# Last head's scores ahead of the output splits, the recurrence in three parts, and two gate products ahead of the memory rows

## The chip, the core and the metric

The kernel runs on one core of one Trainium2 chip. Its engines work side by side, each with a queue that is executed in order: TensorE (PE) multiplies, and PEld is its weight load; VectorE (DVE), ScalarE (ACT) and GpSimd (POOL) work on tiles; SyncE (SP) issues most of the DMAs, ScalarE some. The metric is the time of one execution in microseconds of device time, as the median of several executions. All times below are microseconds unless marked ns.

## What is computed

A sequence of 512 rows of width 1024 (fp32) goes through two blocks, each of two layers.

First block. Layer 0 mixes with dilated attention: 8 heads, and for each head three groups of keys (window and stride 128/1, 512/4, 2048/16) whose outputs are joined by the softmax of their log sums; then a convolving feed-forward network of width 3072. Layer 1 mixes with a gated linear recurrence (RG-LRU) of width 1024, and then has the same kind of network. The recurrence, as the reference has it:

```
r = sigmoid(xr @ ga_w + ga_b);  i = sigmoid(xr @ gx_w + gx_b)
log_a = LRU_C * r * log_sigmoid(lam);  a = exp(log_a)
b = sqrt(max(-expm1(2*log_a), 0)) * i * xb
hs = scan(h_t = a_t*h_(t-1) + b_t);  out = (hs * gelu(gb)) @ w_out
```

Second block, twice: the normed rows are projected, and three branches work on the result: sparse attention of 8 heads (nsa), attention with a decay of 8 heads (fox), and attention over 256 memory rows with 4 heads (memory). Each branch's output goes through a matrix of its own and is multiplied with a sigmoid gate, and the sum goes through a last matrix and is added to the rows:

```
mem_kv = rmsnorm(mem) @ w_mem_kv;  o_m = attention(rmsnorm(q), rmsnorm(k), v) * silu(...)
u = g0*(o_a @ w_branch_a) + g1*(o_b @ w_branch_b) + g2*(o_m @ w_branch_m)
x = x + u @ w_out
```

## The kernel before

Every fp32 matrix product is made of three products of rounded halves (`mm3`, lines 45 to 47): each operand is split into a high part (a cast on ACT) and the rest (a subtraction on DVE), by `split` at line 204. A weight is loaded as 128x1024 values by SP into one of two `ws` tiles and split into one of four pairs `wh`, `wl` (`wunit`, line 212). PSUM is used in four kinds of banks: `acc` (3), `sc` (2), `tr` (2), `pv` (1).

The Python code only sets which instructions there are. A planner orders them on each engine when the program is built, from times that it simulates, so that later work can be pulled into a gap; at run time each queue is in order. `issue_after`, and the helper `behind` around it, tell the planner to place what is written inside the block behind a given instruction on the same engine. `DMA` issues stand in the queue of the engine that issues them.

The three places of the change:

* The end of the attention. `DilatedHead.scores(qk, order)` makes the scores of a head in one of two orders of the rows: four tiles, each with a minimum on DVE (line 109) and an exponential on ACT (line 111). It then writes its statistics to DRAM (`dx<-W`, line 112) and reads the other order's back (`W<-dx`, line 113), both on SP. `normalize` joins the groups (lines 122 to 129) and scales the probabilities on POOL (line 133); `values` transposes them (lines 143, 154) and multiplies with the values. Head 7 is the last: after its scores come the splits of `oT`, the heads' output, for heads 0 to 6 (`hH`, `hL`<-`oT`), the first half of the product with `w_o` (`tm`), and inside it `hold`, which runs `normalize` and `values` of head 7 behind head 6's split and the last weight split.
* The recurrence. `lru_layer` walks `LRU_STEPS`: a number n is `front(n)`, which takes two columns of x from the input product, convolves them (lines 580, 582), splits them, and makes two gates for each (line 722); a range is `recur` over these columns, with Exp and Tanh, then Ln, then Exp on ACT (lines 730, 731, 737, 740) and seven DVE operations a column (lines 744 to 751); each "v" takes one column of gb out of its `acc` bank (line 761). Eight columns of gb in all; the last four stay in their banks till the gelu (line 769), which is placed behind the last Exp of the last recurrence. Then the halves of hs*gate go into the product with `w_out`.
* The start of the second block, in each of its two layers. `memory` loads small vectors, the gain `gm` and the memory rows, norms the rows (lines 309, 312), and takes the four query tiles from `z2`. After two query tiles have been issued, the normed memory rows are transposed (`turned`, line 320) between them; then follow the product with `w_mem_kv` and the four heads. `weave` runs a branch and lets `branch` (gate products of 24 matmuls in two steps, and a product of 12 with the branch's output in one step) fill in, at the steps that `PLANS` lists.

Of the kernel before, what the change touches and what calls it, by code (L numbers as in the profile page):

```python
# [12 lines left out]
AF = mybir.ActivationFunctionType  # L13
OP = mybir.AluOpType
# [4 lines left out]
D = 1024  # L19
NT = T // 128  # L20
KD = D // 128
EPS = 1e-6
NEG = -1e30
BIG = 3e38
# [4 lines left out]
SEC_BUFS = {"st": 7, "ws": 2, "w": 4, "o": 6, "P": 5, "pt": 4, "zc": 3, "hst": 4, "fox_t": 4, "of": 2, "rt": 2, "sl": 2, "mt": 2, "cst": 2, "ct": 2}  # L29
LRU_BUFS = 24  # L30
NORMALIZE_AFTER, VALUES_AFTER = 5, 6
LRU_STEPS = (0, 1, 2, range(4), "v", 3, range(4, 8), "vvv")
PLANS = ((16,),
         (8, 13, 13, 14, 15, 18, 19, 19, 22, 22, 25, 26, 26, 27, 27, 28, 28, 29, 29, 35, 35, 37, 38, 39),
         (1, 5, 5, 8, 8, 10, 12, 15, 16, 17, 19, 21, 32, 32, 34, 35, 38))
TURN_BANKS = (("acc", "sc"), ("acc", "sc"), ("sc", "tr"), ("tr", "pv"))
# [23 lines left out]
class DilatedHead:  # L60
# [23 lines left out]
    def scores(self, qk, order):  # L84
        n, nc = self.n, self.n.nc
        own = self.W[:, order, 0]
        ps = None
        for t in range(NT):
            ts = slice(t * 128, (t + 1) * 128)
            P = self.rows(order, t)  # L90
            N = P.shape[-1]
            if order:

                S = n.bank("sc").rearrange("p (g u c) -> p u g c", g=2, u=2)
                for g in (1, 2):
                    q = qk[g]
                    nc.tensor.matmul(S[:, :, g - 1], q[:, 0, ts], q[:, 2:4, ts], start=True, stop=False)
                    nc.tensor.matmul(S[:, 0, g - 1], q[:, 1, ts], q[:, 2, ts], start=False, stop=True)
                two = lambda x: x.rearrange("p (g c) -> p g c", g=2)
                nc.vector.tensor_tensor(two(P), S[:, 1], two(self.bias[:, 256:512]), op=OP.add)  # L100
                S, bias, P3 = S[:, 0], two(P), two(P)
            else:
                if t % 2 == 0:
                    ps = n.bank("sc")
                S = ps[:, t % 2 * 256:t % 2 * 256 + N]
                q, ks = qk[0], slice((t + 1) * 128 - N, (t + 1) * 128)
                mm3(nc, S, q[:, 0, ts], q[:, 1, ts], q[:, 2, ks], q[:, 3, ks], True, True)
                bias, P3 = self.bias[:, 256 - N:256], P
            nc.vector.tensor_tensor_reduce(out=P3, in0=S, in1=bias, scale=-1.0, scalar=BIG, op0=OP.add, op1=OP.min,
                                           accum_out=own[:, 0, t:t + 1])  # L110
            nc.scalar.activation(P, P, AF.Exp, bias=own[:, 0, t:t + 1], scale=-1.0, accum_out=own[:, 1, t:t + 1])
        nc.sync.dma_start(self.in_dram(order, order), own)
        nc.sync.dma_start(self.W[:, 1 - order, 1], self.in_dram(order, 1 - order))

    def normalize(self):

# [52 lines left out]
class Net:  # L169
# [287 lines left out]
    def dilated_attention(self, qkv, oT):  # L457

        i, ap = self.i, self.ap
        btab = self.btab  # L460
        vectors = self.vectors()
        later, vs, done = [], {}, []
        n = 0

        def after(steps, f, *args):

            later.append((n + steps, f, args))

        def load(hp):
            vs[hp] = self.dilated_values(hp)  # L470

        def values(a):
            a.values(vs[a.hd // 2], a.hd % 2, oT)

        def normalize(a):

            with behind(self.tc, *done):
                a.normalize()

        def due(end=False):  # L480
            for x in [x for x in later if end or x[0] <= n]:
                later.remove(x)
                x[1](*x[2])

        for hd in range(8):
            qk = {}
            a = None
            for g in (1, 2, 0):
                t4 = ap.tile([128, 4, T], F32R, tag="qk", bufs=4, name="qk")
                for u in range(2):  # L490
                    ps = next(qkv)
                    n += 1
# [12 lines left out]
            if hd < 7:  # L505
                after(1, a.scores, qk, 0)
            if hd % 2 == 0:
                after(0, load, hd // 2)
            if hd < 7:
                after(NORMALIZE_AFTER, normalize, a)  # L510
                after(VALUES_AFTER, values, a)
        a.scores(qk, 0)
        due(True)

        def last(ins):
            done[:] = ins
            normalize(a)
            values(a)
        return last

    def first_rows(self, g):

# [23 lines left out]
    def attn_layer(self, g_next, nxt):  # L546
        i, tc = self.i, self.tc
        with tc.tile_pool(name="attO", bufs=1) as self.op, tc.tile_pool(name="attA", bufs=2) as self.ap:
            ap, self.ep = self.ap, self.op
            vs = self.post_vectors(i["norm_mix_post"][0], g_next)  # L550
            self.ep = ap
            oT = self.op.tile([128, KD, T], F32, tag="oT", bufs=1, name="oT")
            last = self.dilated_attention(self.attn_qkv(self.h), oT)
            oh = self.new_h()
            for k in range(KD - 1):
                done = self.split(oh[0][:, k], oh[1][:, k], oT[:, k])

            def hold():
                last((*done, *self.last_split))
                self.split(oh[0][:, KD - 1], oh[1][:, KD - 1], oT[:, KD - 1])  # L560

            free = {}

            def spare(i):
                if i // 4 not in free:
# [222 lines left out]
    def state(self, shape, dt=F32R):  # L788
        return self.lt("st", shape, dt)

    def small_bc(self, row, n, name):
        t = self.lt(name, [128, n])
        self.nc.sync.dma_start(t, row[None, :].to_broadcast([128, n]))
        return t

    def rope_tables(self, g, scale=1.0):
# [160 lines left out]
    def second_layer(self, l, z2):  # L957
        nc, i, tc = self.nc, self.i, self.tc
        w_in, h = i["w_in_2"][l], self.h
        with tc.tile_pool(name=f"sec{l}", bufs=1) as self.lp:  # L960
            lp = self.lp
            u, o_m, o_a, o_b = [], [], [], []
            br = [self.branch(l, h, o, i[f"w_branch_{x}_2"][l], b, u) for o, x, b in ((o_m, "m", 2), (o_a, "a", 0), (o_b, "b", 1))]
            self.weave(self.memory(l, h, w_in, z2, o_m), br[0], PLANS[0])
            self.weave(self.nsa(l, h, w_in, o_a), itertools.chain(br[0], br[1]), PLANS[1])
            self.weave(br[0])
            self.weave(self.fox(l, h, w_in, o_b), itertools.chain(br[1], br[2]), PLANS[2])
# [40 lines left out]
    def branch(self, l, h, o, w, b, u):  # L1008
# [9 lines left out]
        def gate(m):  # L1018
# [1 line left out]
            wh, wl = self.wunit(wg[:, :, c:c + 128])  # L1020
            pg = self.bank()
            for k in range(KD):
                mm3(nc, pg, wh[:, k], wl[:, k], h[0][:, k], h[1][:, k], k == 0, k == KD - 1)
                if k == KD // 2 - 1:
                    yield
            t = self.lt("mt", [128, T])
# [347 lines left out]
            nc.sync.dma_start(K[o:o + 2, e::2], self.cd[1, :, 4 * hf + e:4 * hf + 4:2])  # L1374


    def memory(self, l, h, w_in, z2, os):
        nc, i, lp = self.nc, self.i, self.lp
        lh, ll = self.rows(h)
        gq = self.small_bc(i["mem_q_norm_2"][l], 128, "gq")  # L1380
        gk = self.small_bc(i["mem_k_norm_2"][l], 128, "gk0")
        gm = self.lt("pt", [128, D])
        nc.sync.dma_start(gm, i["mem_norm_g_2"][l][None, :].to_broadcast([128, D]))
        mH, mL = self.state([128, KD, 256]), self.state([128, KD, 256])
        rows = []
        for t in range(2):
            mt, xn = self.lt("pt", [128, D]), self.lt("o", [128, D])
            nc.sync.dma_start(mt, i["mem_2"][0, t * 128:(t + 1) * 128])
            rows.append(self.normed(mt, gm, (xn[:, :512], xn[:, 512:], xn)))
        Q = [self.state([128, 2, 2, T]) for _ in range(2)]  # L1390
        for t, ps in enumerate(z2):
            if t >= 2:
                self.turned(rows[t - 2], (mH, mL), t - 2)
            cs = slice(t * 128, (t + 1) * 128)
            for c in range(2):
                zc = self.lt("zc", [128, 256])
# [1 line left out]
                qn = self.head_norm(zc, 2, 128)  # L1398
                nc.vector.scalar_tensor_tensor(qn, qn, 128 ** -0.5, gq[:, None, :].to_broadcast([128, 2, 128]), op0=OP.mult, op1=OP.mult)
                pt = self.transposed([qn[:, a] for a in range(2)])  # L1400
                self.split(Q[c][:, 0, :, cs], Q[c][:, 1, :, cs], pt[:, :256].rearrange("p (h q) -> p h q", h=2))
            yield
        wkv = i["w_mem_kv_2"][l]
        mlh, mll = self.rows((mH, mL))
        K = self.state([128, 2, 4, 256])
# [136 lines left out]
```

## Time and profile before

| | |
|---|---|
| Median of 3 runs | 2842.91 (2842.14 to 2843.55) |
| The profiled execution | 2847.33 |
| Its span, from the first to the last instruction | 2845.2 |
| PE busy | 2752.4 (97%), 14493 matmuls |
| DVE, ACT, POOL busy | 1655.0 (58%), 1285.5 (45%), 509.2 (18%) |
| Mean granted clock of TensorE | 0.988 of full speed |

The profile is of one execution. Busy time of an engine is the time in which at least one of its instructions ran; consecutive matmuls overlap in it, so a matmul's duration is longer than its distance to the next. A row names the line of the kernel, the engine, the operation, and what it writes and reads (`hH<-oT`).

### The profile page before, as it was taken

To read this page: it belongs to the slowest core of one execution; us is meant where nothing else is said; L and a number is where in the kernel's file an instruction comes from. 1 tells how busy PE (TensorE), PEld (TensorE's weight loads), DVE (VectorE), ACT (ScalarE), POOL (GpSimd) and SP (SyncE) were. 2 spreads that over 40 slices of the span, in tenths; PEclk is the share of its full clock that TensorE was granted. 3 is DMA by queue.
4 is the path that set the end of the run, shared out by engine and by line. 5 is a ranking of instruction groups with operands and counts; after the bars stand their busy time and mean duration, and the time that the engine had idled before them with its cause. 6 is when DMAs were issued, how large, how long until landed. Compare 5 with 4: busy or idle time off the path is not lost.

```text
span 2845.2 us, 39405 instructions
## 1 busy us (share of the span) xinstructions
PE 2752.4 (97%) x14493; PEld 2338.7 (82%) x14493; DVE 1655.0 (58%) x3306; ACT 1285.5 (45%) x2518; POOL 509.2 (18%) x682
## 2 busy tenths in 40 slices
PE   7999999799999998999998999999999899999999
PEld 6788888688888887888887898789878798788987
DVE  3245555555542678555425687776744677777753
ACT  3234344344432465444323554666533554665542
POOL 0001101111100000111001242333320242333420
PEclk9999999899999999999999999999999999999999
DMA  5553443333332343433323424122234423113233
GB/s 172 171 169 86 104 94 86 118 111 97 97 126 96 112 122 108 126 96 97 126 97 114 125 74 109 38 54 75 71 93 141 137 70 109 34 46 84 71 93 107
DMA packets 386071, 288.52 MB, mean 101 GB/s; under 512 B 33576, under 2 KB 339496, under 8 KB 385880
## 3 DMA queue, kind: packets, MB, share of 16 engines
q1 hardware_dynamic: 376752, 268.94, 32.9%
q10 hardware_dynamic: 9128, 17.07, 1.6%
q8 instruction: 115, 1.88, 0.3%
q14 instruction: 76, 0.62, 0.1%
HBM read 266.86 MB, written 21.20 MB: 101 GB/s over the span
## 4 chain that ended last, share of the span: by engine, by line
PE 82%; DVE 8%; DMA 4%; ACT 3%; issue 2%; POOL 1%; SPq 0%; ACTq 0%; DVEq 0%; POOLq 0%
PE acc L45 20%; PE acc L46 20%; PE acc L47 20%; PE tr L856 2%; PE sc L45 2%; PE sc L46 2%; PE sc L47 2%; DVE wl L204 2%; PE pv L916 2%; PE tr L45 2%; PE tr L47 1%; PE tr L46 1%; PE pv L46 1%; PE pv L47 1%; DMA ws<-in_attn_w_qkv_dram 1%
## 5 line engine op out<-in xcount | busy, mean ns | idle before, releaser
L204 DVE TENSOR_TENSOR wl<-ws,wh 128x1024 fp32r<-128x1024 f32 (+2 forms) x476 | 563.9, 1186 | 686.8 <-ACT wh L204 680.8
L204 ACT CAST wh<-ws 128x1024 fp32r<-128x1024 f32 (+2 forms) x476 | 469.5, 987 | 819.7 <-PE acc L46 303.6
L45 PE MATMUL acc<-hH,wh 128*128 128x512 f32 (+1 forms) x1928 | 742.3, 386 | 12.2 <-ACT gate L769 6.2
L46 PE MATMUL acc<-hL,wh 128*128 128x512 f32 (+1 forms) x1928 | 741.3, 385 | 1.5 <-DVE hL L204 1.2
L47 PE MATMUL acc<-hH,wl 128*128 128x512 f32 (+1 forms) x1928 | 739.5, 384 | 1.0 <-DVE wl L204 1.0
L45 PEld LDWEIGHTS acc<-hH,wh 128*128 128x128 f32 x1928 | 363.3, 189 | 83.6 <-ACT gate L769 6.6
L47 PEld LDWEIGHTS acc<-hH,wl 128*128 128x128 f32 x1928 | 363.9, 189 | 69.2 <-DVE wl L204 1.5
L46 PEld LDWEIGHTS acc<-hL,wh 128*128 128x128 f32 x1928 | 364.1, 189 | 68.4 <-DVE hL L204 2.5
L45 PE MATMUL acc<-wh,hH 128*128 128x256 f32 (+3 forms) x864 | 267.3, 312 | 5.4 <-ACT hH L204 4.1
L46 PE MATMUL acc<-wl,hH 128*128 128x256 f32 (+3 forms) x864 | 266.9, 310 | 2.3 <-DVE wl L204 2.3
L47 PE MATMUL acc<-wh,hL 128*128 128x256 f32 (+3 forms) x864 | 264.9, 309 | 0.1
L45 PEld LDWEIGHTS acc<-wh,hH 128*128 128x128 f32 x864 | 165.6, 192 | 14.5 <-ACT hH L204 4.5
L46 PEld LDWEIGHTS acc<-wl,hH 128*128 128x128 f32 x864 | 165.7, 192 | 11.9 <-DVE wl L204 3.7
L47 PEld LDWEIGHTS acc<-wh,hL 128*128 128x128 f32 x864 | 165.3, 191 | 7.4 <-DVE hL L204 0.4
L645 POOL TENSOR_TENSOR cv<-cv 128x512 f32<-128x512 f32 x48 | 62.0, 1292 | 465.1 <-DVE cv L582 448.4
L582 DVE SCALAR_TENSOR_TENSOR cv<-acc,cw,cv 128x511 f32<-128x511 f32 (+1 forms) x192 | 142.5, 746 | 3.2
L856 PE MATMUL tr<-ident,P 128*128 128x128 f32 x720 | 123.3, 277 | 10.7 <-DVE pt L204 5.2
L817 POOL TENSOR_TENSOR hst<-hst,mhalf 128x4 f32<-128x4 f32 (+2 forms) x90 | 91.0, 1017 | 223.5 <-DVE hst L816 221.7
L889 ACT ACTIVATE P<-P,soft 128x128 f32<-128x128 f32 (+1 forms) x192 | 108.1, 563 | 49.9 <-DVE soft L888 45.7
L888 DVE CUSTOM_DVE_ANT_0 P<-sc,causal 128x128 f32<-128x128 f32 (+1 forms) x192 | 92.9, 486 | 45.8 <-PE tr L856 31.5
L891 POOL TENSOR_SCALAR P<-P,soft,ngate 128x128 f32<-128x128 f32 (+3 forms) x128 | 83.9, 658 | 153.6 <-DVE soft L890 117.5
L204 DVE TENSOR_TENSOR pt<-tr,pt 128x128 fp32r<-128x128 f32 (+2 forms) x224 | 104.1, 474 | 11.8 <-ACT pt L204 10.4
(452 smaller groups left out, 4770.1 us busy)
## 6 DMA issues: line engine op xcount, KB each, us to landing
ws<-in_w_in_dram SPq DMA_DIRECT2D x116, 512.0 KB
ws<-in_ffn_w_up_dram SPq DMA_DIRECT2D x96, 512.0 KB
ws<-in_attn_w_qkv_dram SPq DMA_DIRECT2D x72, 512.0 KB
ws<-in_ffn_w_down_dram SPq DMA_DIRECT2D x48, 512.0 KB
x<-x ACTq DMA_DIRECT2D x16, 512.0 KB
ws<-in_lru_w_in_dram SPq DMA_DIRECT2D x16, 512.0 KB
ws<-in_w_mem_kv_dram SPq DMA_DIRECT2D x16, 512.0 KB
ws<-in_w_out_dram SPq DMA_DIRECT2D x16, 512.0 KB
```

The lines of the kernel that those rows point to most:

```text
L45: nc.tensor.matmul(out, lh, rh, start=start, stop=False)
L46: nc.tensor.matmul(out, lh, rl, start=False, stop=False)
L47: return nc.tensor.matmul(out, ll, rh, start=False, stop=stop)
L204: return nc.scalar.copy(hi, src), (eng or nc.vector).tensor_tensor(lo, src, hi.bitcast(F32), op=OP.subtract)
L582: nc.vector.scalar_tensor_tensor(dst[:, s:], ps[:, :T - s], cw(taps - 1 - s), dst[:, s:], op0=OP.mult, op1=OP.add)
L645: nc.gpsimd.tensor_tensor(g, g, v, op=OP.mult)
L817: nc.gpsimd.tensor_tensor(st[:, 1], st[:, 0], self.mhalf[:rows, :nh], op=OP.pow)
L856: self.nc.tensor.transpose(ps[:, a * 128:(a + 1) * 128], s, self.ident)
L888: nc.vector.tensor_tensor_reduce(out=P, in0=S, in1=self.causal[:, 512 - n:512], scale=-1.0, scalar=BIG, op0=OP.add, op1=OP.min, accum_out=m)
L889: nc.scalar.activation(P, P, AF.Exp, bias=m, scale=-1.0, accum_out=s)
L891: nc.gpsimd.tensor_scalar(P, P, r, mult, op0=OP.mult, op1=OP.mult)
L916: nc.tensor.matmul(ps[:, lo:256], v(j), p[:, j, lo:], start=first and j == 0 and u == 0, stop=last and j == nj - 1 and u == 1)
```

## The change

1. `LRU_STEPS` runs three recurrences (columns 0 to 3 after the second front, 4 and 5 after the third, 6 and 7 after the fourth) in place of two (0 to 3 after the third front, 4 to 7 after the fourth). The columns of the input product keep their order.
2. The splits of `oT` of heads 0 to 6 are placed behind the last minimum and the last exponential of head 7's scores. `normalize` of head 7 is placed behind the split of head 6 alone. Head 7's two reads `W<-dx` are issued by POOL in place of SP.
3. In `memory` the two small vectors, the two tiles of memory rows and `gm` are loaded from ACT's queue in place of SP's, the rows ahead of `gm`. The rows are normed behind the last split of the queries, and transposed behind the last matmul of the second gate product: four steps of `branch` (two gate products of 24 matmuls) are run between the queries and the memory rows. The one fill step inside the memory branch (at its step 16) goes; the other plans stay, so that each finds the branch three steps further on.

```diff
-LRU_STEPS = (0, 1, 2, range(4), "v", 3, range(4, 8), "vvv")
-PLANS = ((16,),
+LRU_STEPS = (0, 1, range(4), 2, range(4, 6), "v", 3, range(6, 8), "vvv")
+PLANS = ((),
...
-            nc.vector.tensor_tensor_reduce(out=P3, in0=S, in1=bias, scale=-1.0, scalar=BIG, op0=OP.add, op1=OP.min,
-                                           accum_out=own[:, 0, t:t + 1])
-            nc.scalar.activation(P, P, AF.Exp, bias=own[:, 0, t:t + 1], scale=-1.0, accum_out=own[:, 1, t:t + 1])
+            ends = (nc.vector.tensor_tensor_reduce(out=P3, in0=S, in1=bias, scale=-1.0, scalar=BIG, op0=OP.add, op1=OP.min,
+                                                   accum_out=own[:, 0, t:t + 1]),
+                    nc.scalar.activation(P, P, AF.Exp, bias=own[:, 0, t:t + 1], scale=-1.0, accum_out=own[:, 1, t:t + 1]))
         nc.sync.dma_start(self.in_dram(order, order), own)
-        nc.sync.dma_start(self.W[:, 1 - order, 1], self.in_dram(order, 1 - order))
+        (nc.gpsimd if self.hd == 7 else nc.sync).dma_start(self.W[:, 1 - order, 1], self.in_dram(order, 1 - order))
+        return ends
...
-            for k in range(KD - 1):
-                done = self.split(oh[0][:, k], oh[1][:, k], oT[:, k])
+            with behind(tc, *ends):
+                for k in range(KD - 1):
+                    done = self.split(oh[0][:, k], oh[1][:, k], oT[:, k])
...
-                last((*done, *self.last_split))
+                last(done)
...
-            self.weave(self.memory(l, h, w_in, z2, o_m), br[0], PLANS[0])
+            self.weave(self.memory(l, h, w_in, z2, o_m, br[0]), br[0], PLANS[0])
...
-        for t in range(2):
-            mt, xn = self.lt("pt", [128, D]), self.lt("o", [128, D])
-            nc.sync.dma_start(mt, i["mem_2"][0, t * 128:(t + 1) * 128])
-            rows.append(self.normed(mt, gm, (xn[:, :512], xn[:, 512:], xn)))
         Q = [self.state([128, 2, 2, T]) for _ in range(2)]
         for t, ps in enumerate(z2):
-            if t >= 2:
-                self.turned(rows[t - 2], (mH, mL), t - 2)
...
+        for n in range(4):
+            next(fill)
+        with behind(self.tc, *ends):
+            rows = []
+            for mt in mts:
+                xn = self.lt("o", [128, D])
+                rows.append(self.normed(mt, gm, (xn[:, :512], xn[:, 512:], xn)))
+        with behind(self.tc, self.last_gate):
+            for t in range(2):
+                self.turned(rows[t], (mH, mL), t)
```

## Rows read from the trace of the kernel before

**Rows 1.** The page, its first part: busy time, share of the span, instructions.

```profile
PE 2752.4 (97%) x14493; PEld 2338.7 (82%) x14493; DVE 1655.0 (58%) x3306; ACT 1285.5 (45%) x2518; POOL 509.2 (18%) x682
```

**Rows 2.** Waits of PE: who was waited for, us in total, times, longest.

```profile
PE tr L143 <- POOL PA L133: 7.0, 1, 7.0
...
PE acc L320 <- ACT o L309: 4.3, 1, 4.3
...
PE acc L320 <- DVE o L312: 3.4, 1, 3.4
```

**Rows 3.** Busy time (x instructions) of PE, PEld, DVE, ACT, POOL by stretch; clock; DMA.

```profile
480.00:535.00 55.00, 42.26 (x208) 35.46 (x208) 26.11 (x55) 20.09 (x44) 3.76 (x9) 0.84 0.25 77
...
1020.00:1070.00 50.00, 48.80 (x214) 39.78 (x214) 38.41 (x56) 40.94 (x55) 0.00 (x0) 1.00 0.44 136
1070.00:1085.00 15.00, 8.79 (x31) 6.76 (x30) 14.82 (x22) 12.07 (x20) 0.00 (x0) 0.77 0.26 89
...
1549.00:1566.00 17.00, 9.11 (x28) 6.44 (x27) 12.90 (x36) 8.42 (x23) 6.28 (x9) 0.60 0.29 104
...
2203.00:2218.00 15.00, 8.53 (x34) 6.35 (x33) 11.58 (x33) 9.00 (x23) 6.65 (x9) 0.77 0.39 119
```

**Rows 4.** Timeline at the attention's end: start, us, engine, line, what.

```profile
479.17 0.93 PE L143 MATMUL tr<-ident,PA 128*128 128x128 f32 x7
480.80 0.45 PE L45 MATMUL acc<-wh,hH 128*128 128x512 f32 x1
...
479.44 2.17 ACT L204 CAST hH<-oT 128x512 fp32r<-128x512 f32 x4
...
483.50 0.68 DVE L204 TENSOR_TENSOR qk<-acc,qk 128x512 fp32r<-128x512 f32 x1
...
495.38 0.49 ACT L111 ACTIVATE PA<-PA,W 128x256 f32<-128x256 f32 x1
...
496.00 0.37 SPq L112 DMA_DIRECT2D dx<-W  x1
505.65 0.36 SPq L113 DMA_DIRECT2D W<-dx  x1
...
509.74 0.17 DVE L122 TENSOR_TENSOR c<-W 128x8 f32<-128x8 f32 x1 [4.08 <-DMA W<-dx]
...
512.33 0.21 ACT L125 ACTIVATE c<-c 128x16 f32<-128x16 f32 x1
...
514.60 1.74 POOL L133 TENSOR_SCALAR PA<-PA,c 128x128 f32<-128x128 f32 x4 [34.41 <-DVE c L129]
...
515.03 2.06 PE L143 MATMUL tr<-ident,PA 128*128 128x128 f32 x7 [7.00 <-POOL PA L133]
```

**Rows 5.** Timeline of the recurrence, on ACT, DVE and PE.

```profile
1023.50 1.28 ACT L730 ACT_TABLE_LOAD   x1
...
1052.91 2.93 ACT L730 ACTIVATE a<-th,lrul 128x512 f32<-128x512 f32 x4
...
1072.67 1.28 ACT L769 ACT_TABLE_LOAD   x1
1073.97 2.19 ACT L769 ACTIVATE gate<-gate 128x512 f32<-128x512 f32 x4
...
1041.42 0.68 DVE L761 COPY gate<-acc 128x512 f32<-128x512 f32 x1
...
1076.69 0.79 PE L45 MATMUL acc<-hH,wh 128*128 128x512 f32 x1 [6.21 <-ACT gate L769]
```

**Rows 6.** Timeline of the first memory branch's start, on SP and PE.

```profile
1549.89 0.91 SPq L1388 DMA_DIRECT2D pt<-in_mem_dram  x2
...
1560.58 0.78 PE L45 MATMUL acc<-wh,hH 128*128 128x512 f32 x1
...
1565.42 0.52 PE L47 MATMUL acc<-wh,hL 128*128 128x512 f32 x1
```

**Rows 7.** Timeline of the fox branch's end, on PE.

```profile
2091.00 0.95 PE L45 MATMUL acc<-o,wh 128*128 128x512 f32 x2 [2.29 <-ACT o L204]
```

More of the change, by code (lines that the diff above doesn't have):

```diff
@@ L511, in dilated_attention @@
                 after(VALUES_AFTER, values, a)
-        a.scores(qk, 0)
+        ends = a.scores(qk, 0)
         due(True)
@@ L518, in last @@
             values(a)
-        return last
+        return last, ends
     def first_rows(self, g):
@@ L552, in attn_layer @@
             oT = self.op.tile([128, KD, T], F32, tag="oT", bufs=1, name="oT")
-            last = self.dilated_attention(self.attn_qkv(self.h), oT)
+            last, ends = self.dilated_attention(self.attn_qkv(self.h), oT)
             oh = self.new_h()
-            for k in range(KD - 1):
-                done = self.split(oh[0][:, k], oh[1][:, k], oT[:, k])
+            with behind(tc, *ends):
+                for k in range(KD - 1):
+                    done = self.split(oh[0][:, k], oh[1][:, k], oT[:, k])
             def hold():
-                last((*done, *self.last_split))
+                last(done)
                 self.split(oh[0][:, KD - 1], oh[1][:, KD - 1], oT[:, KD - 1])
@@ L789, in state, with small_bc @@
         return self.lt("st", shape, dt)
-    def small_bc(self, row, n, name):
+    def small_bc(self, row, n, name, eng=None):
         t = self.lt(name, [128, n])
-        self.nc.sync.dma_start(t, row[None, :].to_broadcast([128, n]))
+        (eng or self.nc.sync).dma_start(t, row[None, :].to_broadcast([128, n]))
         return t
@@ L1022, in gate @@
             for k in range(KD):
-                mm3(nc, pg, wh[:, k], wl[:, k], h[0][:, k], h[1][:, k], k == 0, k == KD - 1)
+                self.last_gate = mm3(nc, pg, wh[:, k], wl[:, k], h[0][:, k], h[1][:, k], k == 0, k == KD - 1)
                 if k == KD // 2 - 1:
@@ L1374, in decay_keys, with memory @@
             nc.sync.dma_start(K[o:o + 2, e::2], self.cd[1, :, 4 * hf + e:4 * hf + 4:2])
-    def memory(self, l, h, w_in, z2, os):
+    def memory(self, l, h, w_in, z2, os, fill):
         nc, i, lp = self.nc, self.i, self.lp
         lh, ll = self.rows(h)
-        gq = self.small_bc(i["mem_q_norm_2"][l], 128, "gq")
-        gk = self.small_bc(i["mem_k_norm_2"][l], 128, "gk0")
+        gq = self.small_bc(i["mem_q_norm_2"][l], 128, "gq", nc.scalar)
+        gk = self.small_bc(i["mem_k_norm_2"][l], 128, "gk0", nc.scalar)
         gm = self.lt("pt", [128, D])
-        nc.sync.dma_start(gm, i["mem_norm_g_2"][l][None, :].to_broadcast([128, D]))
+        mts = [self.lt("pt", [128, D]) for _ in range(2)]
+        for t in range(2):
+            nc.scalar.dma_start(mts[t], i["mem_2"][0, t * 128:(t + 1) * 128])
+        nc.scalar.dma_start(gm, i["mem_norm_g_2"][l][None, :].to_broadcast([128, D]))
         mH, mL = self.state([128, KD, 256]), self.state([128, KD, 256])
-        rows = []
-        for t in range(2):
-            mt, xn = self.lt("pt", [128, D]), self.lt("o", [128, D])
-            nc.sync.dma_start(mt, i["mem_2"][0, t * 128:(t + 1) * 128])
-            rows.append(self.normed(mt, gm, (xn[:, :512], xn[:, 512:], xn)))
         Q = [self.state([128, 2, 2, T]) for _ in range(2)]
         for t, ps in enumerate(z2):
-            if t >= 2:
-                self.turned(rows[t - 2], (mH, mL), t - 2)
             cs = slice(t * 128, (t + 1) * 128)
@@ L1400, in memory @@
                 pt = self.transposed([qn[:, a] for a in range(2)])
-                self.split(Q[c][:, 0, :, cs], Q[c][:, 1, :, cs], pt[:, :256].rearrange("p (h q) -> p h q", h=2))
+                ends = self.split(Q[c][:, 0, :, cs], Q[c][:, 1, :, cs], pt[:, :256].rearrange("p (h q) -> p h q", h=2))
             yield
+        for n in range(4):
[6 more added lines that the diff above has]
+        with behind(self.tc, self.last_gate):
+            for t in range(2):
+                self.turned(rows[t], (mH, mL), t)
         wkv = i["w_mem_kv_2"][l]
```

## The prediction

> **What bounds the kernel.** I read the page first. PE is busy for 2752.4 of the span's 2845.2 us [rows 1], so it is the bound, and the change removes no matmul: it can win only idle time of PE, 92.8 us in all, and what PE loses at the lower clock after a gap. Next, PE's waits, sorted [rows 2]: 7.0 us for POOL's normalize of head 7 (line 133), and 4.3 and 3.4 us for the memory rows' norm (lines 309, 312). Then the stretches around the three edited places [rows 3]. Each line's length less PE's busy time is its idle time: 12.74 us at the attention's end, 6.21 behind the last recurrence, 7.89 and 6.47 at the two starts of the memory branch; together 33.3 of the 92.8 us. In the same lines the granted clock is 0.84, 0.77, 0.60 and 0.77: in part of each stretch PE ran at the lower of its two levels, 1.2 instead of 2.4 GHz. At full clock one matmul of 512 columns comes every 0.228 us (48.80 us for 214 of them) [rows 3]; behind the first memory gap twelve come from 1560.58 to 1565.42, 0.44 us apart [rows 6]; seven transposes take 0.93 us before the attention's gap and 2.06 behind it [rows 4]. The timelines [rows 4 to 6] say what each gap waited for.
>
> **A, the attention's end.** The chain: head 7's last exponential at 495.38, the write of its statistics issued at 496.00, the read issued when that had landed, at 505.65 (9.65 us), VectorE's first use at 509.74 (4.08 us), the joint exponential on ScalarE only at 512.33, POOL at 514.60, PE at 515.03 after 7.00 us of idling [rows 4]. The scores could have been earlier: ScalarE cast four parts of oT (2.17 us from 479.44) before the last query was split, and PE ran the output product from 480.80, well before the last exponentials [rows 4]. With the splits behind the scores, the queries are split by 484.2 at the latest (483.50 + 0.68), and four minima and exponentials of some 0.6 us follow: the end comes near 486.6, 9.3 us earlier. The remaining chain, 514.60 - 495.87 = 18.7 us, would end at 505.3; of the 2.6 us between VectorE's first use and the joint exponential, part goes too, as the wait on the weight split is dropped. I take POOL at 504.
>
> PE's work between 480.80 and 508.03 (515.03 - 7.00) isn't removed, only started later, so it still ends near 508 or later, and the normalize is then ready: the 7.0 us go. So does the half clock behind them: over 55 us a mean of 0.84 is 17.6 us at half rate, of which at most 12.7 are idle; the other 4.9 us of work cost 2.4. Of the remaining 5.7 us of idling, in head 6's and head 7's hand-offs, I take a third, since head 6's come before the product now. Against this, PE has no product to run from 480.80 until the scores are done and a first part of oT is split: between nothing, if head 6's transposes and values and head 7's scores fill that, and 5.9 us, the whole way to 486.7. I take 1.5, since head 6's values are ready to run there. Sum: -7.0 - 2.4 - 1.9 + 1.5 = **-9.8** (from -15.1, all of the stretch's idling and clock, to -5.4).
>
> Moved DMAs: SyncE no longer holds the read of head 7, so the weight loads queued behind it are not held for 9.65 us. POOL issues both reads and is blocked while it waits for the writes; behind them on POOL stands only head 7's own normalize (POOL idles for 34.41 us before it [rows 4]). No transfer issued by POOL is in this trace. Bounds by the nearest rows: 4.08 us, as from SyncE, and 9.65, as the slowest of these small transfers. Nearest is the same transfer at 4.08; up to 4 us more are hidden, as POOL would be ready at 504 and PE not before 508. The Trainium skill speaks against this move (SBUF — State Buffer, its "DVE blocks DMA" trap): VectorE can lock GpSimd out while it writes descriptors, and a DMA of 620 ns took 3100. By that the read would be some 2.5 us later, which the 4 us still cover.
>
> **B, the recurrence.** The last input column waited for a bank that the gelu had to free: PE idled 6.21 us until 1076.69 [rows 5]. The gelu stands behind the second recurrence, which took from 1052.91 to 1072.67, 19.8 us for four columns with two table loads of 1.28 [rows 5]. For two columns: (19.8 - 2.6)/2 + 2.6 = 11.2 us, ending at 1064.1. With the gelu's load (1.28), four gelus (2.19) and one from PSUM (0.55) the bank is free at 1068.1; PE asks for it at 1070.48 (1076.69 - 6.21). The gap goes, and with it the half clock: 31 matmuls at 0.228 are 7.1 us against 8.79 busy, 1.7 us. Added: one more recurrence, two more table loads, 2.6 us of ScalarE. They lie in the stretch before 1070, where ScalarE is busy for 40.94 and VectorE for 38.41 of 50 us and PE still 48.80 [rows 3]; the first recurrence moves ahead by one front, into emptier time. I take 1.4 us of new short waits of PE (the idling of that line is 1.2). Sum: -6.2 - 1.7 + 1.4 = **-6.5** (from -7.9 to 0). A load's end and the next activation lie 0.02 us apart (1072.67 + 1.28, and the gelu at 1073.97 [rows 5]). The Trainium skill (ScalarE: Activation LUTs, What ACT_TABLE_LOAD costs) adds 1.38 us of drain to each load of 1.28, which would make the two loads 5.3 us; the trace doesn't agree, and the sum has none of it.
>
> **C, the memory branch, twice.** In the first layer SyncE issues the rows at 1549.89, and PE runs the third query tile only at 1560.58, behind the first transposed row [rows 6]. With the pins the third and fourth tiles (48 matmuls, 10.9 us) and two gate products (48 more, 10.9 us) come first, 21.9 us from about 1550, and the row's chain (load, norm: 10 us in this trace) lies under them. Gone: 7.89 us idle and 11 x (0.44 - 0.228) = 2.3 of clock; in the second layer 6.47, and half as much clock, 1.2, as the mean shows 3.5 us of full rate missing against 6.8. Together -17.9.
>
> Costs, for each layer: the rows are normed only behind the last query, so a rest of waiting of 1 us (0 to 2) before the transposes. Five DMA issues, 0.45 us each by SyncE's row (0.91 for two [rows 6]), leave SyncE's queue, where only weight loads and the next branch's small vectors stand behind them, and enter ScalarE's; behind them wait the casts of the last rows and those that free the query banks, for 2.3 us at most, and PE has 5.5 us of the third tile over them: counted in that rest. The fill step inside the memory heads is gone: 12 matmuls, 2.7 us of cover, 1 taken (0 to 2.7). And the three steps now run early are missing at the end: 36 matmuls, 8.2 us. Fox's last heads are filled with what is left of the gates, and at their end PE already waits 2.29 us for the last output [rows 7]. Where the cover lacks, softmax chains show: 0 to 8.2, I take 3, near the 2.29 us that PE idles there already. Sum: -17.9 + 2 x (1 + 1 + 3) = **-7.9** (from -17.9 to +7.9).
>
> **Sum.** -9.8 - 6.5 - 7.9 = -24.2, on the profiled execution's 2847.3 (span 2845.2 and 2.1 around it): 2823.1. The median of the runs is 4.4 below that execution, so 2818.7: **2819**.
>
> **Rivals.** *1. The filler is only lent:* fox's end lacks all of it, and C comes to nothing: 2819 + 8 = 2827. For it: the 2.29 us wait [rows 7] shows that filler runs out. Against: it is the only wait of that size I found there. Chance 0.17. *2. POOL's read is late:* descriptors written on a busy POOL take 4 + 7 us more, PE's 7.0 us gap stays and A falls to about -1: 2828. For it: no row shows such a transfer. Against: VectorE, which could be in POOL's way, is busy for only 26.11 of 55 us there [rows 3]. Chance 0.06. This is where the trap that the Trainium skill describes (SBUF — State Buffer) would end. *3. The planner puts it otherwise:* it orders by simulated times, and gets the rows' load wrong before (it put the transposes ahead of the third query tile, 10 us too early). If two of the three gaps reappear in another place, some 17 of the 24 us are lost: 2836. Chance 0.10. *4. Slower: the recurrences come ahead of the columns.* Place: 1003 to 1070. The recurrences of the first four columns (19.8 us, as the second took for four [rows 5]) and of the next two (11.2) both get ahead of the convolutions that free the banks of later columns; the three banks fill, and PE stops for up to 31 us less one column in hand (24 matmuls, 5.5 us), in place of B: -24.2 + 6.5 + 25.5 = +8, 2851. It ends slower than before from 18 us of new idling there. Against: a gate column is taken out at 1041.42 amid the first recurrence [rows 5], so the planner did not put evacuations last. Chance 0.07.
>
> **Numbers.** My case has 0.60, with 2808 to 2830 of its own. Range 2804 to 2837: the low end is two thirds of the way from my sum to all the best bounds (-40.9, 2802); the high end holds rivals 1 to 3 and leaves out 4. A measurement here tells 0.2% (5.7 us) from no change, so faster means below 2837.2: my case, rivals 1 and 2, and half of rival 3: 0.88; same 0.05; slower 0.07.
>
> **What would show it.** A: the write of head 7's statistics near 487, POOL ready before PE's transposes, no 7 us wait on line 133, clock 1.00 past 515. B: no wait of line 45 on the gelu, three groups of Ln with two more table loads, last Exp near 1064. C: PE without a gap over 2 us from the first query tile to the memory product, the norm's waits gone from PE's list. Wrong it would be if PE's waits in fox's last steps grow by over 5 us a layer, if a wait on POOL's read stands before the transposes of head 7, or if PE waits on convolutions between 1003 and 1070.

## The result: slower by 1.1%, and the profile after

| | before | after |
|---|---|---|
| Median of the runs | 2843.23 (2842.14 to 2844.61) | 2874.84 (2872.62 to 2876.86) |
| Ratio, with its 95% interval | | 1.0111 (1.0093 to 1.0128) |
| The profiled execution, its span | 2847.33, 2845.2 | 2876.12, 2874.3 |

The forecast was 2819, with 2804 to 2837: wrong in sign. The page after, the line that answers to [rows 1]:

```profile
PE 2759.1 (96%) x14493; PEld 2344.4 (82%) x14493; DVE 1656.9 (58%) x3306; ACT 1290.5 (45%) x2520; POOL 521.8 (18%) x684
```

The same 14493 matmuls take 6.7 us more, and the rest of the 29.1 us by which the span grew is new idle time of PE: 115.2 us in place of 92.8. PE's waits after, sorted (us in total, times, longest), answer to [rows 2]:

```profile
PE acc L45 <- ACT zc L1395: 13.6, 6, 4.3
...
PE acc L321 <- DVE o L313: 6.8, 4, 3.2
...
PE tr L858 <- DVE zc L1397: 4.4, 2, 2.2
...
PE tr L858 <- DVE st L205: 4.3, 2, 2.1
...
PE acc L45 <- ACT wh L205: 3.5, 2, 2.3
...
PE tr L45 <- ACT xh L205: 3.1, 1, 3.1
```

The 7.0 us wait for POOL is gone, as forecast, and of the 6.2 us for the gelu 1.6 are left, in three short waits. The first four lines are of the memory branch's start: new are the waits on the queries (lines 1395 and 1397 copy and scale them, and a split frees their bank), while those on the norm of the rows (line 313) have replaced 4.3 and 3.4 us on the same norm before [rows 2]. The longest waits of the last two lines are of the recurrence. The stretches that answer to [rows 3]:

```profile
478.00:533.00 55.00, 46.07 (x231) 38.80 (x229) 27.80 (x59) 21.71 (x49) 8.89 (x14) 0.91 0.29 89
...
1014.00:1040.00 26.00, 20.37 (x80) 15.61 (x79) 26.00 (x39) 17.30 (x25) 0.00 (x0) 0.87 0.42 132
...
1064.00:1079.00 15.00, 14.32 (x63) 11.54 (x62) 11.62 (x19) 12.90 (x20) 0.00 (x0) 1.00 0.21 70
1541.00:1583.00 42.00, 26.29 (x105) 20.10 (x105) 24.26 (x54) 18.34 (x40) 8.69 (x11) 0.82 0.35 118
2209.00:2255.00 46.00, 32.62 (x138) 25.43 (x136) 23.78 (x54) 18.29 (x40) 8.70 (x11) 0.84 0.37 120
```

At the attention's end PE idles for 8.9 us of 55 instead of 12.7. Behind the last recurrence 0.7 us are left of 6.2, but 1014 to 1040 is a new hole of 5.6. In that hole VectorE is busy for all 26 us. The two memory starts are the loss: 15.7 and 13.4 us idle, at a clock of 0.82 and 0.84.

**Attention's end after** (answers to [rows 4]): the last exponential, the write and the read of its statistics, VectorE's first use, POOL, PE.

```profile
490.30 0.49 ACT L111 ACTIVATE PA<-PA,W 128x256 f32<-128x256 f32 x1
...
490.91 0.37 SPq L112 DMA_DIRECT2D dx<-W  x1
501.10 0.72 POOL L113 DMA_DIRECT2D W<-dx  x1 [11.54 <-DMA dx<-W]
504.53 0.17 DVE L123 TENSOR_TENSOR c<-W 128x8 f32<-128x8 f32 x1 [7.73 <-DMA W<-dx]
506.28 3.82 POOL L134 TENSOR_SCALAR PA<-PA,c 128x128 f32<-128x128 f32 x4 [4.46 <-ACT wh L205]
...
510.88 0.92 PE L144 MATMUL tr<-ident,PA 128*128 128x128 f32 x7
```

PE comes to the transposes without a wait, 0.8 us after POOL's last scaling of PA.

**Recurrence after** (answers to [rows 5]), ScalarE, VectorE and PE some 40 us ahead of the old gap, and ScalarE's last exponential:

```profile
1017.15 0.77 ACT L582 ACTIVATE xb<-acc,lrucv 128x512 f32<-128x512 f32 x1
...
1022.10 0.74 DVE L584 SCALAR_TENSOR_TENSOR xb<-acc,lrucv,xb 128x511 f32<-128x511 f32 x1
...
1025.17 0.74 DVE L584 SCALAR_TENSOR_TENSOR xb<-acc,lrucv,xb 128x510 f32<-128x510 f32 x1
...
1026.38 1.04 ACT L205 CAST wh<-ws 128x1024 fp32r<-128x1024 f32 x1 [1.76 <-DMA ws<-in_lru_w_in_dram]
...
1027.48 0.50 PE L45 MATMUL acc<-hH,wh 128*128 128x512 f32 x1 [2.32 <-ACT wh L205]
...
1027.63 1.21 DVE L753 TENSOR_TENSOR_SCAN th<-a,th 128x512 f32<-128x512 f32 x1
...
1029.35 0.74 DVE L584 SCALAR_TENSOR_TENSOR xb<-acc,lrucv,xb 128x509 f32<-128x509 f32 x1
...
1029.99 0.81 ACT L733 ACTIVATE th<-th,lrul 128x512 f32<-128x512 f32 x1
...
1030.69 0.61 ACT L205 CAST xh<-xb 128x512 fp32r<-128x512 f32 x1
...
1031.35 0.79 PE L45 MATMUL tr<-xh,wh 128*128 128x512 f32 x1 [3.14 <-ACT xh L205]
...
1066.14 1.16 ACT L742 ACTIVATE y<-y 128x512 f32<-128x512 f32 x2
```

PE waits 2.32 us for a weight and 3.14 us for the split of a convolved column. That column's convolution began on ScalarE at 1017.15 (line 582, 580 before); its three steps on VectorE (line 584) come at 1022.10, 1025.17 and 1029.35, with the first recurrence's operations (line 753 is its scan) between them. A tanh of the second recurrence (line 733) then holds the split back for another 0.6 us.

**First memory start after** (answers to [rows 6]):

```profile
1543.08 1.39 ACTq L1388 DMA_DIRECT2D pt<-in_mem_norm_g_dram  x1
1544.51 0.92 ACT L1395 COPY zc<-acc 128x256 f32<-128x256 f32 x3 [2.86 <-DMA gq<-in_mem_q_norm_dram]
...
1545.21 0.49 PE L45 MATMUL acc<-wh,hH 128*128 128x512 f32 x1 [2.61 <-ACT zc L1395]
...
1554.07 1.04 ACT L205 CAST wh<-ws 128x1024 fp32r<-128x1024 f32 x1 [4.73 <-DMA ws<-in_w_mem_kv_dram]
...
1555.71 0.80 PE L45 MATMUL acc<-hH,wh 128*128 128x512 f32 x1 [4.30 <-ACT zc L1395]
...
1573.95 0.41 PE L858 MATMUL tr<-ident,zc 128*128 128x128 f32 x2 [2.15 <-DVE st L205]
...
1576.58 0.66 PE L858 MATMUL tr<-ident,zc 128*128 128x128 f32 x2 [2.21 <-DVE zc L1397]
1577.27 0.37 ACT L205 CAST st<-tr 128x256 fp32r<-128x256 f32 x1 [2.50 <-PE tr L858]
1577.54 1.06 ACT L310 ACTIVATE o<-pt 128x1024 f32<-128x1024 f32 x1
...
1580.44 1.09 PE L321 MATMUL acc<-ident,o 128*128 128x128 f32 x4 [3.21 <-DVE o L313]
```

Read it from the end. The rows' norm (line 310) begins at 1577.54, right behind the last query's split at 1577.27, which is what the pin asks for. That split comes so late since each query tile goes through ScalarE, VectorE, GpSimd, PE and ScalarE again, and PE has nothing left to run in between: the gate products are over, and the memory product waits for the rows. Ahead of that, PE stands twice for a bank that a query's copy on ScalarE has to free: 2.61 us, where ScalarE is busy issuing the five loads, and 4.30 us, where it waits 4.73 for a weight that the planner put ahead of the copy; a third such wait, at 1565.61, is 1.01.

**Time at equal work.** The order of the matmuls differs behind 1541, so I count each matmul of a trace with what it takes at full clock (0.227 us for 512 columns, 0.088 for a transpose, from the trace before) and compare when the same sum is reached. Against the trace before, the kernel after loses, in the first layer and the second, +10.1 and +8.5 us at the memory branch's start and +8.9 and +9.0 us behind it, to the layer's end. With the 7.4 us won ahead of the first of these starts that is the 29.1 us by which the span grew.

### The profile page after: what moved, and what is told of

The parts are those of the page before. It is cut to its first block, busy times and chain, and to the rows that moved or that the text cites. A ratio compares the mean times of both kernels' runs of the same rounds, so it can differ in the third digit from the quotient of the medians.

```text
span 2874.3 us, 39426 instructions
## 1 busy us (share of the span) xinstructions
PE 2759.1 (96%) x14493; PEld 2344.4 (82%) x14493; DVE 1656.9 (58%) x3306; ACT 1290.5 (45%) x2520; POOL 521.8 (18%) x684
## 4 chain that ended last, share of the span: by engine, by line
PE 82%; DVE 8%; ACT 4%; DMA 4%; issue 2%; POOL 1%; ACTq 0%; SPq 0%; DVEq 0%; POOLq 0%
PE acc L45 20%; PE acc L46 20%; PE acc L47 20%; PE tr L858 2%; DVE wl L205 2%; PE sc L46 2%; PE sc L45 2%; PE sc L47 2%; PE pv L918 2%; PE tr L46 1%; PE tr L47 1%; PE tr L45 1%; ACT wh L205 1%; PE pv L46 1%; PE pv L47 1%
## 5 line engine op out<-in xcount | busy, mean ns | idle before, releaser
L205 DVE TENSOR_TENSOR wl<-ws,wh 128x1024 fp32r<-128x1024 f32 (+4 forms) x476 | 571.1, 1201 | 718.0 <-ACT wh L205 713.2
L205 ACT CAST wh<-ws 128x1024 fp32r<-128x1024 f32 (+4 forms) x476 | 469.6, 987 | 830.9 <-PE acc L46 318.1
L45 PEld LDWEIGHTS acc<-hH,wh 128*128 128x128 f32 x1928 | 363.5, 189 | 89.0 <-ACT zc L1395 11.2
```

The lines of the kernel that those rows point to most:

```text
L45: nc.tensor.matmul(out, lh, rh, start=start, stop=False)
L205: return nc.scalar.copy(hi, src), (eng or nc.vector).tensor_tensor(lo, src, hi.bitcast(F32), op=OP.subtract)
```

## Experiments

Ratios are to the kernel before, run on the same chip between the others. "Start" and "rest" are us won (-) or lost (+) at equal work, first layer and second, as above; from trace to trace a "rest" in which nothing was changed moves by some 4 (e1: -0.4 and -3.4; e5: -4.1 and -4.0). A trace is of one execution: that of e7 took 5.7 us less than the median of its kernel, that of e6 7.6 us more.

**The parts apart.** In e1 the memory branch is as before; in e2 only the memory branch is changed; in e3 only the attention's end; in e12 only `LRU_STEPS`.

```diff
-LRU_STEPS = (0, 1, 2, range(4), "v", 3, range(4, 8), "vvv")
+LRU_STEPS = (0, 1, range(4), 2, range(4, 6), "v", 3, range(6, 8), "vvv")
```

> The attention's end and the three recurrences as changed, the memory branch as before. My theory: the loss lies in the memory branch alone, and the other two parts win what the trace after the change shows at equal counts of matmuls, 5.3 and 1.2 us: 2843.2 - 6.5 = 2836.7, ratio 0.9977. Rival (what the first two parts move costs later, by other slots of the weights' tiles): 2843 or more.

> The memory branch's start as changed, the attention and the recurrence as before. My theory: the whole loss is here, some 37 to 39 us for both layers: 2843.2 + 38 = 2881, ratio 1.013. Rival (the parts act on each other, the order found behind the changed recurrence makes the memory branch bad): clearly less, under 2865.

> The attention's end alone as changed. By the trace at equal counts of matmuls it wins 5.3 us: 2838, ratio 0.9981, and the recurrence's three parts are the 1.2 us between this and the run of both. Rival (my prediction's sizes): 9.8 us, 2833.4, and the recurrence alone 6.5.

> The three recurrences alone, attention and memory as before. The run of the first two parts won 0.19% (0.10 to 0.28), the attention alone 0.00% (-0.08 to 0.09). If they add, the recurrence wins 0.19%, some 5 us (2838); by the trace at equal work of TensorE it wins 1.3 us only (ratio 0.9995), since the 6.2 us wait on the gelu gave way to waits of 1.5, 3.4 and 0.7 us ten columns earlier with TensorE at half clock behind them. My prediction had 6.5.

| | ratio | 95% interval |
|---|---|---|
| e1, attention and recurrence | 0.9981 | 0.9972 to 0.9990 |
| e2, memory alone | 1.0133 | 1.0120 to 1.0147 |
| e3, attention alone | 1.0000 | 0.9992 to 1.0009 |
| e12, recurrence alone | 1.0001 | 0.9992 to 1.0009 |

The loss is all in the memory branch: +1.33% alone (38 us), and 1.0111 - 0.9981 = 1.30% on top of the other parts. The other two win 5.4 us together (2.8 to 8.0), and neither can be told from nothing alone, so the run of both is at the edge of what the two single runs allow. By counts of matmuls (the orders agree there), from the 2000th to the 2750th the attention's end is 4.7 us shorter in e1's trace, 5.6 in the trace after, 1.6 in e3's; from the 4500th to the 5250th the recurrence wins 1.3, 1.3 and, in e12's, 2.0.

**ScalarE's loads, and the pin of the norms.** e4 puts the five loads back on SyncE; e7 norms the rows without the pin; e9 does both.

```diff
-            nc.scalar.dma_start(mts[t], i["mem_2"][0, t * 128:(t + 1) * 128])
+            nc.sync.dma_start(mts[t], i["mem_2"][0, t * 128:(t + 1) * 128])
...
-        with behind(self.tc, *ends):
-            rows = []
-            for mt in mts:
+        rows = []
+        for mt in mts:
```

> The kernel after the change, but the five loads of each memory branch (two small vectors, the rows, the gain) are issued from SyncE's queue again, in the order of the change. Theory 1 (ScalarE's queue is held by the issues, 3 us, and the query's copies and what frees the banks comes late by them): the wait of 2.6 us at the third query tile goes, some 3 us a layer, 2874.8 - 6 = 2869. Theory 2 (it is the pins and the two gate products ahead of the rows, which make one serial chain of what lay in parallel): no difference beyond 2 us, 2873 to 2877.

> The kernel after the change, but the rows are normed as soon as they are there, not behind the last split of the queries; the gate products stay ahead of them and the transposes behind the second of these. Theory 1 (the pin makes the row's chain of norm and transposes serial behind the last query): the waits of 3.2 us on the norm goes with part of what is ahead of it, some 4 us a layer: 2867. Rival (the chain of the last two query tiles on ScalarE, VectorE and GpSimd is what the transposes wait for, whichever comes first): 2873 to 2877.

> The kernel after the change with the rows normed as soon as they are there and the five loads issued from SyncE's queue again; the gate products stay ahead of the transposes. If ScalarE's issues cost what the run with loads from SyncE showed beside the change (0.2%), and the pin's cost is a thing apart: 0.2% under the run with the norm not pinned, ratio 1.001, 2848. Rival (ScalarE has room again once the norms are not pinned): no difference, 1.003.

| | ratio | 95% interval | start | rest |
|---|---|---|---|---|
| after | 1.0111 | 1.0093 to 1.0128 | +10.1, +8.5 | +8.9, +9.0 |
| e4, loads from SyncE | 1.0090 | 1.0074 to 1.0105 | +3.6, +2.7 | +11.8, +11.0 |
| e7, norms not pinned | 1.0031 | 1.0020 to 1.0042 | -2.5, -2.5 | +5.8, +6.3 |
| e9, both | 1.0005 | 0.9996 to 1.0015 | -2.0, -3.5 | +7.0, +4.5 |

The pin costs 0.80% (22.8 us), far more than the 4 us a layer that I expected of it. The loads cost 0.21% beside the pin and 0.26% without it, some 6 to 7 us; the two intervals of e4 and of the kernel after overlap, those of e7 and e9 don't. With the norm free, e7's chain is under the cover as the change meant it:

```profile
1552.45 1.06 ACT L310 ACTIVATE o<-pt 128x1024 f32<-128x1024 f32 x1 [3.30 <-DMA pt<-in_mem_dram]
...
1570.86 0.60 PE L321 MATMUL acc<-ident,o 128*128 128x128 f32 x4
```

The rows are normed as they land, 25 us earlier than after the change, and their transposes begin with no wait behind the second gate product. The query's last transposes run inside the memory product.

**The pin alone** (e15): the first two parts, no gate product ahead, loads from SyncE; of the third part only `behind(self.tc, *ends)` around the norms and, as that asks for, their transposes behind the fourth query tile.

> The first two parts of the change; of the third the pin alone: rows normed behind the last split of the queries, transposed behind that, no gate product ahead, loads from SyncE in the old order. Theory (the pin makes the whole chain of the last query tiles a condition of the memory product, some 11 us a layer): 2841.6 + 20 = 2862 beside a run before of 2847, ratio 1.004 to 1.006. Rival (the pin is harmless without ScalarE's loads and without the gate products): within 0.1% of the run of the first two parts, 0.997 to 0.999.

Measured: 1.0044 (1.0030 to 1.0057), 0.63% or 17.9 us over e1; start +10.5 and +7.1, rest -1.6 and 0.0. The theory holds: the pin needs neither the loads nor the gate products to do harm. Nor is it the later place of the transposes: e13 below has both rows' transposes behind the fourth tile too, without the pin and with its loads in another order, and measured 0.9989, 0.55% less. The timeline of e15:

```profile
1548.03 0.94 SPq L1389 DMA_DIRECT2D pt<-in_mem_dram  x2
...
1562.91 0.66 PE L858 MATMUL tr<-ident,zc 128*128 128x128 f32 x2 [7.53 <-DVE zc L1397]
...
1572.01 1.06 ACT L310 ACTIVATE o<-pt 128x1024 f32<-128x1024 f32 x1
...
1574.92 1.09 PE L321 MATMUL acc<-ident,o 128*128 128x128 f32 x4 [3.21 <-DVE o L313]
```

The loads are issued at 1548.03, the norm begins at 1572.01; between them PE waits 7.53 us at one place for the query's chain alone.

**The lent gate products.** e5 is the kernel after without them (with the fill step inside the memory heads back, and no pin of the transposes); e6 is the first two parts with them alone; e10 is e9 with the first three entries of the next plan taken out, so that each later entry finds the gate branch where it did before. One edit of each, in this order:

```diff
-        for n in range(4):
-            next(fill)
...
+PLANS = ((3, 3, 3, 3),
...
-         (8, 13, 13, 14, 15, 18, 19, 19, 22, 22, 25, 26, 26, 27, 27, 28, 28, 29, 29, 35, 35, 37, 38, 39),
+         (14, 15, 18, 19, 19, 22, 22, 25, 26, 26, 27, 27, 28, 28, 29, 29, 35, 35, 37, 38, 39),
```

> The kernel after the change without the two gate products ahead of the memory rows (the fill step inside the memory heads is back, as before); the pins of the rows behind the queries and the loads from ScalarE stay. At equal work of TensorE the trace after the change loses in each layer about 10 us at the memory branch's start and about 9 in the two branches behind it. Theory 1 (the 9 are the lent filler): these come back in both layers, 18 us, and the start costs about what it did: 2874.8 - 18 = 2857. Theory 2 (the gate products are the cover that the pinned rows need, the filler's loss is small): the start gets worse by what they covered, up to 10.9 us each, and it is no faster than 2875.

> The first two parts of the change, and of the third nothing but two gate products run behind the last query tile (by the plan of fill steps); rows, pins and loads as before. Theory 1 (lent filler costs 9 us a layer): 2841.6 + 18 = 2860, less what the products hide at the start, 0 to 6 a layer: 2848 to 2860. Theory 2 (the loss is in the pins and the loads): within 5 us of the run of the first two parts alone, 2837 to 2847.

> The same kernel, and the plan of fill steps of the sparse branch loses its first three entries (8, 13, 13), so that every later entry finds the gate branch at the step that it found before the change. Theory (the time lost behind the memory branch, 16 to 19 us for both layers by the run of the gate products alone, comes from other steps standing at the planned places, not from too few of them: as many are left as before, only the bare rest at the end is shorter): the loss goes but for the cover at the three places, 36 matmuls at 0.228 us or 8.2 us a layer at most and 2 likely: ratio 0.9955 to 0.998, 2833 to 2840. Rival (any step that is lent is missed where it is taken, wherever that is): 1.001 as the run beside it.

| | ratio | 95% interval | start | rest |
|---|---|---|---|---|
| e5, after without them | 1.0049 | 1.0034 to 1.0064 | +11.2, +9.5 | -4.1, -4.0 |
| e6, they alone | 1.0047 | 1.0032 to 1.0062 | -0.5, -1.6 | +13.1, +9.6 |
| e10, e9 with the plan shifted | 0.9998 | 0.9989 to 1.0007 | -5.3, -2.3 | +7.0, +5.4 |

Lending costs 0.62% by e5 and 0.66% by e6, 18 to 19 us, and all of it in the branches behind. In e6 it hides nothing at the start, since the rows' transposes still stand ahead of it, with their wait of 4.31 us for the norm. e10's theory falls: shifting the plan back moves the loss and doesn't lessen it. Where the three entries are missing, early in the sparse branch, 7.2 us at equal work are lost at once in the first layer, near the 8.2 that 36 matmuls take; nothing is lost behind it. That stretch in the kernel before:

```profile
1765.00:1795.00 30.00, 26.31 (x155) 20.98 (x153) 25.56 (x101) 20.97 (x63) 14.67 (x23) 1.00 0.20 54
```

And in e10, PE's busy time is 2.8 us less and its clock 0.83:

```profile
1758.00:1788.00 30.00, 23.49 (x123) 18.02 (x122) 23.39 (x96) 19.07 (x58) 14.49 (x22) 0.83 0.11 27
```

In e9, which keeps the entries, the same sum is lost in smaller pieces, near 1720, 1780, 1900 to 1950 and 2100. Why a step that stands three places further on covers less there, I did not settle.

**Candidates.** e8: the first two parts, and each row's transposes one query tile later, with no pin and nothing lent. e14: the same with the loads in the order first row, gain, second row. e13: that, and both rows behind the fourth tile.

```diff
-            if t >= 2:
-                self.turned(rows[t - 2], (mH, mL), t - 2)
+            if t >= 3:
+                self.turned(rows[t - 3], (mH, mL), t - 3)
...
+        self.turned(rows[1], (mH, mL), 1)
```

> The first two parts of the change, and the memory branch as before but with each row's transposes one query tile later in the program (between the third and the fourth tile, and behind the fourth), with no pin and no gate product. If the idle time at the start before (7.9 and 6.5 us) came from the transposes standing ahead of the third query tile, the third tile covers some 5 us of it in each layer: 2841.6 - 8 = 2834. Rival: it moves to the wait for the second row or the query's banks, and nothing is won: 2839 to 2844.

> A candidate: the first two parts, rows transposed one query tile later, no pin, no gate product lent, and the memory rows loaded by SyncE ahead of the gain and of the second small vector (first row, gain, second row). The first row's load is issued some 0.9 us earlier; what is left of waits on the norm in the run without that order is 0.9 and 2.8 us in the first layer, 0.5 and 1.5 in the second: I expect 1 to 3 us less than there, ratio 0.9965. Rival: the gain, which every norm needs, lands last and sets the same end: 0.9974.

> The same with both rows' transposes behind the fourth query tile. If the waits on the norm are the rest, both tiles cover them and it wins 2 us more: 0.996. Rival (the fourth tile waits for a bank that the query's copies free, and then the memory product for the rows' splits): 0.998 or more.

Measured: e8 0.9974 (0.9963 to 0.9986), start -1.3 and -1.1; e14 0.9991 (0.9982 to 1.0000); e13 0.9989 (0.9980 to 0.9998). e8 beats both kernels, but not e1 by more than the intervals. The other two miss: the start is no better in the second layer (+1.7, +1.8), and some 5 us are lost behind it there, for which I have no cause. Idle time at the start, which the change meant to fill, comes back as other waits on the norm or the queries whichever way the rows are put: the most that any kernel here won of it is 5.3 and 3.5 us a layer, with the gate products as cover.

## Why the prediction was wrong

**C failed, at the sentence "the rows are normed only behind the last query, so a rest of waiting of 1 us (0 to 2) before the transposes".** It measured 12.6 and 11.0 us (start after less start in e7: 10.1 + 2.5, 8.5 + 2.5), and 10.5 and 7.1 with the pin alone (e15). I compared the 21.9 us of cover with the rows' own chain, 10 us of load and norm. With the pin that chain begins only behind the last query's split, which starts at 1577.27, and what has to fit under the cover is the chain of all four query tiles plus the norm. The trace before had the numbers: there the first query transposes run at 1553 and the last at 1583, 13 us into the memory product. I never asked when the last split falls. In e7, without the pin, the row's chain does lie under the cover.

**The cover itself was not 21.9 us of free work.** The tile that PE runs at 1560.58 in the trace before was read as the third of the queries; it is the fourth. PE's busy time (x instructions) of matmuls into the `acc` banks there, with clock and DMA:

```profile
1531.50:1550.10 18.60, 17.21 (x72) 1.00 0.54 171
1561.00:1569.00 8.00, 7.81 (x24) 0.71 0.22 58
```

A tile is 24 matmuls: three had run ahead of the gap, one was left behind it, so there were 72 matmuls of cover, 16.4 us, and not 96. "PE has 5.5 us of the third tile over them": what was left, the fourth tile, was itself waiting for the bank that ScalarE, busy with the issues, had to free (2.61 us), and the first gate product for the next (4.30). Beside the pin the two gate products were worth about 1 us of the start in each layer (e5: +11.2 and +9.5 without them). So the gain of 17.9 us was mis-sized too: with the pin gone 5.0 (e7) to 7.6 us (e10) are won at the two starts. The loads on ScalarE cost 6 to 7 us where I had them inside the 1 us. The Trainium skill (DMA: Bandwidth & Descriptors, Rules for kernel authors) says that spreading DMAs over the issuing engines saves only issue time; here it moved 3 us of it to the one queue that PE was waiting for.

**The filler.** I had 1 + 3 us a layer, with the loss at fox's end. It is 9 a layer (e5, e6), above even the 8.2 that rival 1 ("only lent") put as the most, and the place was right in part only. At fox's end (2062 to 2112 and 2722 to 2770 of the trace before) PE loses 2.4 and 2.8 us at equal work, near the 3 of the sum (the runs that lend nothing, e1, e5 and e15, lie between -1.4 and +1.5 there). Some 7 us more in each layer, which the sum had at nothing, lie all along the two branches ahead of that place: each plan still issues as many steps as before, but other ones, and what gets shorter is the bare rest at the very end, where nothing needs cover.

**A: the mechanism was right, the size was not.** The 7.0 us wait went. But the scores ended at 490.8, not 486.6: the last query is split by 481.9, even before the 484.2 that I gave, but six exponentials follow it and not four, with head 6's values between their scores on PE, and PE waits there (0.42, 1.76 and 1.49, together 3.7, in place of my 1.5). Behind the transposes 0.62 and 0.96 are new. The half clock did not go reliably. All kernels but e2 and e12 have this part, with the same order of matmuls; in their traces it wins between 0.7 (e14) and 7.3 us (e10) by counts of matmuls, and the granted clock tells these two apart. The stretch in e14:

```profile
478.00:533.00 55.00, 45.39 (x215) 38.85 (x214) 26.30 (x58) 18.48 (x40) 11.49 (x18) 0.82 0.29 88
```

And in e10:

```profile
478.00:533.00 55.00, 46.35 (x238) 38.69 (x238) 29.89 (x67) 21.55 (x49) 11.01 (x18) 0.94 0.29 90
```

PE's wait for the first split behind the transposes is 1.51 us in e14 and under 0.4 in e10, each followed by one of about 0.96. Rival 2 didn't come: POOL's read was used 3.4 us after its issue, against 4.08 from SyncE, so no trace here shows the trap of the Trainium skill (SBUF — State Buffer). Nor was it put to the test: VectorE stood idle for 7.73 us, till 504.53, while that read was issued and landed.

**B: rival 4 in small.** The gap behind the last recurrence went with its half clock, as worked out. "1.4 us of new short waits" measured 4.4 (5.6 idle in 1014 to 1040, where the trace before has 1.2 in 1022 to 1048), and the clock fell to 0.87. The place is the one that rival 4 named, a recurrence ahead of a convolution, though not its full stop. The first recurrence did not move "into emptier time": it met the convolution on VectorE, which is busy for 26.00 of 26 us there, and 17.70 in the stretch of the trace before:

```profile
1022.00:1048.00 26.00, 24.80 (x109) 19.91 (x108) 17.70 (x29) 22.11 (x30) 0.00 (x0) 1.00 0.48 152
```

Of the 6.5 us, by counts of matmuls, -0.2 (e13) to 2.0 (e12) are left in the traces of the kernels that have this part.

Sum: A and B were forecast at -16.3 and measured -5.4; C at -7.9 and measured +37. The chance of 0.07 for slower hung on a mechanism in B alone; the pin had no rival of its own. The range's low end, 2804, is nine tenths and not two thirds of the way from 2819 to 2802; nothing hung on it.

## What to carry to other kernels

An instruction placed behind the last one of a chain inherits the whole chain: read from the trace when that last one ends and what PE still has to run by then, not only how long the pinned work is. Cover only counts if its own inputs and banks don't come from the chain that it is to hide. Fill steps moved ahead are missing or differently placed somewhere else, and cost there about what they take on PE.

## What the runs showed of the hardware

- One issue of the gain's DMA took 1.39 us in ScalarE's queue in the first layer (1.38 to 1.39 in e2, e5 and e7) and 0.44 in the second, against 0.43 in SyncE's queue before; the trace shows no reason.
- POOL's four scalings took 3.82 us after and 1.74 before [rows 4]. After the change two weight splits on VectorE (2.36 us from 506.20) run beside them. Head 6's four, with one such split (1.23 us) beside them, took 2.77 in both traces. The Trainium skill (SBUF — State Buffer, two separate sides) has VectorE with two operands in SBUF and GpSimd exclude each other for an instruction at a time, which would fit; no run tested it.
- The write of the statistics took 9.3 (e10) to 10.7 us (e1) from its issue to the read's, 9.65 before: moving the read to another queue left that alone, and it is now what sets POOL's start.
